# A convolution's tiles moved from GpSimd to VectorE in a two-layer hybrid network on one core

## The chip, the cores and the metric

The kernel runs on one core of one Trainium2 chip, as one launch. The metric is the device time of that launch in microseconds (us), shown as the median of several runs. A profile comes from one execution of its own; its span runs from the first to the last instruction.

## The reference, cut to what matters

The network has two layers over 256 tokens of width 2048, all in float32. The first mixes retention and a sparse attention; the second mixes a depthwise convolution of 31 taps over 1024 channels and an attention over three dilation patterns. The change touches three pieces: the input norm, the convolution and the norm of each head of 128 (`dilated_attention` norms dq and dk so):

```python
def rms_norm(x, gain):
    y = xf * lax.rsqrt(jnp.mean(xf * xf, axis=-1, keepdims=True) + NORM_EPS)
    return y * gain

def conformer_conv(u, g, dw_w, dw_b, ln_g, ln_b):
    a = u * jax.nn.sigmoid(g)
    a = lax.conv_general_dilated(a, dw_w[:, None, :], (1,), [(CONV_K - 1, 0)],
            dimension_numbers=('NWC', 'WIO', 'NWC'), feature_group_count=C) + dw_b
...
def odd_layer(x, norm_g, w_in, ...):
    h = rms_norm(x, norm_g) @ w_in
    cu, cg, cz, dq, dk, dv, dz = split_cols(h, ODD_SPLITS)
    c_out = conformer_conv(cu, cg, ...) * silu(cz)
    d_out = dilated_attention(dq, dk, dv, dil_qn, dil_kn) * silu(dz)
    return x + jnp.concatenate([c_out, d_out], axis=-1) @ w_out
```

## The kernel before, in words

Nearly all of the work is projections: `project` multiplies the normed input, 2048 deep, by 512 columns of weights, in chunks of 512 rows. float32 accuracy is had from three products of two halves: each chunk comes in by one DMA as raw (1 MB), and `prep` (line 92) splits it in two half-chunks of 128x1024, each into an upper part wh, copied by ScalarE (line 104), and a lower part wl, which VectorE subtracts (line 105). TensorE then does wh by xh, wl by xh and wh by xl. Each of raw, wh and wl has three buffers. A half-chunk feeds 24 matmuls of 256 columns (the transposed form, `flip=True`, lines 134 to 136) or 12 of 512 columns (lines 140 to 142). A project of the second layer has four chunks, so eight wh and eight wl.

The input is kept transposed as xT (channels by tokens). `norm_block` (lines 178 to 189) makes its two halves xh and xl, ScalarE and VectorE one instruction for each 256 columns. The root of each token's mean square is not put into them, but into the projections' results: for the first layer `token_rstd` gives rstd1, which `evac_to` (line 266) applies when ScalarE copies a result out of PSUM. Its sums of squares come from `input_squares` (lines 208 to 218), which loads the input a second time, laid out by token (xtok, four DMAs of 512 KB), and lets ScalarE square and sum it. For the second layer they come from `square_block` (lines 191 to 197): a square of four rows of xT on ScalarE and a reduction on VectorE over every 256th element (line 197); `token_squares` adds the four blocks and sums over the channels by two matmuls of one column.

The second layer runs in this order: two projects for the gate and the input of the first four channel tiles of the convolution (cg, cu), two for the second four, six for the queries and keys of the dilated attention (here d projects: d00, d10, d01, d11, d02, d12), three for its values (dv), then three gates and the output. In line 779 GpSimd multiplies input and gate into apad, with 30 zeros ahead, and from then on the first half's convolution can run, beside the projects that follow; the second half's after the fourth project.

`conv` (lines 731 to 754) takes a channel tile and a stretch of taps. Of every four tiles (ct % 4) the first two go to VectorE: one `scalar_tensor_tensor` a tap (line 744) that adds a weighted, shifted apad to a sum in PSUM (cps), each tile in a bank of its own, copied out by ScalarE at the end (line 746). For the other two ScalarE makes the weighted copy (tap, three buffers, line 753) and GpSimd adds it to acc in SBUF (line 754). Tap 0 is written straight into the sum (lines 742, 750). `conv_pieces` cuts a half into 16 pieces of four taps each, of one VectorE tile and one ScalarE/GpSimd tile:

```python
        def piece(i, k):
            def f():
                for ct in (4 * hf + i, 4 * hf + i + 2):
                    conv(ct, k, min(k + CONV_STEP, CONV_K))
            return f
        return [piece(i, k) for i in range(2) for k in range(0, CONV_K, CONV_STEP)]
```

The pieces stand in a list, and `take(range(3))` gives a project one piece after each of its first three chunks. What is left when the last value project has been issued is issued then.

After each d project `head_norm` (lines 269 to 284) squares it on ScalarE, sums each head on VectorE (line 275), has GpSimd make the roots (`rsqrt`, lines 166 to 171) and scales: by VectorE in one multiplication, or, with `act=True`, as for the six d projects, by ScalarE in eight copies of 128 columns (line 281). Then TensorE transposes it (line 293) in two groups of four.

Each engine works its queue in order. The order within it is set by a scheduler that places instructions by its own estimate of times; the weights' loads, splits and evacuations have high priority (`tc.high_priority`), so that the taps fill in between.

Of the kernel before, what the change touches and what calls it, by code (L numbers as in the profile page):

```python
# [33 lines left out]
DILS = (1, 4, 16)  # L34
MMB = 3
WARM = 36
CONV_STEP = 4
HPO = 2000


# [20 lines left out]
def hybrid_kernel(ctx: ExitStack, tc: tile.TileContext, a: dict, out: bass.AP):  # L61
# [143 lines left out]
            nc.tensor.matmul(pt[:, t:t + 1], tot[:, t * 128:(t + 1) * 128], ones, start=True, stop=True)  # L205
        return pt[:, :2]

    def input_squares():

        ss = st.tile([128, 16], F32, name="xss", tag="ss")  # L210
        for t in range(2):
            for c in range(2):
                xt = hp.tile([128, 1024], F32, name="xtok", tag="h")
                nc.sync.dma_start(xt, a["xtok"][:, t, 1024 * c:1024 * c + 1024])
                nc.scalar.activation(xt, xt, AF.Square, accum_out=ss[:, 2 * t + c:2 * t + c + 1])
        tot = st.tile([128, 2], F32, name="xtot")
        nc.vector.reduce_sum(tot, ss[:, :4].rearrange("p (t c) -> p t c", t=2), axis=AX.X)
        return tot

    def token_rstd(tot, name):  # L220

        ms = st.tile([128, 16], F32, name=name + "m", tag="ms")
        nc.vector.tensor_scalar(ms[:, :2], tot, 1.0 / D, EPS, op0=ALU.mult, op1=ALU.add)  # L223
        r = const.tile([128, 2], F32, name=name)
        nc.gpsimd.tensor_tensor(r, ms[:, :2], mhalf[:, :2], op=ALU.pow)  # L225
        return r
# [39 lines left out]
            nc.scalar.activation(dst[:, t, off:off + n], p[:, :n], AF.Copy, scale=r[:, t:t + 1])  # L266
        return f

    def head_norm(view, nh, name, act=False):

        sq = sp.tile([128, 1024], F32, name="sq", tag="sq")
        sqv = sq[:, :2 * nh * 128].rearrange("p (t h d) -> p t h d", t=2, h=nh)
        nc.scalar.activation(sqv, view, AF.Square)
        ss = st.tile([128, 16], F32, name=name + "ss", tag="ss")
        nc.vector.reduce_sum(ss[:, :2 * nh], sq[:, :2 * nh * 128].rearrange("p (g d) -> p g d", d=128), axis=AX.X)
        rs = rsqrt(ss[:, :2 * nh], 2 * nh, HD, name + "rs")
        if act:
            for t in range(2):
                for h in range(nh):
                    i = t * nh + h  # L280
                    nc.scalar.activation(view[:, t, h, :], view[:, t, h, :], AF.Copy, scale=rs[:, i:i + 1])
            return
        rb = rs.rearrange("p (t h) -> p t h", t=2).unsqueeze(3).to_broadcast([128, 2, nh, 128])
        nc.vector.tensor_mul(view, view, rb)

# [19 lines left out]
    def first_block(c):  # L305
        load_block(c)
        if c == 3:
            rstd.append(token_rstd(input_squares(), "rstd1"))

    project(ew[0], 512, lhs, evac_to(hkv), lazy=first_block, cut=load_rest)  # L310
    load_pack("pa")
# [419 lines left out]
    def conv(ct, k0, k1):  # L731


        src, dst = apad[ct // 4][:, ct % 4, :], acc[ct // 4][:, ct % 4, :]
        w, b = dww[:, ct, :], dwb[:, ct:ct + 1]
        if ct % 4 < 2:
            if ct % 4 == 0 and k0 == 0:
                cps[0] = ps.tile([128, 1024], F32, name="cps", tag="sc")
            p = cps[0][:, 512 * (ct % 4):512 * (ct % 4) + S]
            for k in range(k0, k1):  # L740
                if k == 0:
                    nc.vector.tensor_scalar(p, src[:, 0:S], w[:, 0:1], b, op0=ALU.mult, op1=ALU.add)
                else:
                    nc.vector.scalar_tensor_tensor(p, src[:, k:k + S], w[:, k:k + 1], p, op0=ALU.mult, op1=ALU.add)  # L744
            if k1 == CONV_K:
                nc.scalar.copy(dst, p)
            return
        for k in range(k0, k1):
            if k == 0:
                nc.scalar.activation(dst, src[:, 0:S], AF.Identity, scale=w[:, 0:1], bias=b)  # L750
                continue
            tap = sp.tile([128, S], F32, name="tap", tag="tap", bufs=3)
            nc.scalar.activation(tap, src[:, k:k + S], AF.Copy, scale=w[:, k:k + 1])  # L753
            nc.gpsimd.tensor_add(dst, dst, tap)  # L754

    def conv_pieces(hf):
        def piece(i, k):
            def f():
                for ct in (4 * hf + i, 4 * hf + i + 2):
                    conv(ct, k, min(k + CONV_STEP, CONV_K))  # L760
            return f
        return [piece(i, k) for i in range(2) for k in range(0, CONV_K, CONV_STEP)]

    apad, acc = [], []
    for hf in range(2):
# [60 lines left out]
    for p_ in range(3):  # L826
        for i in range(2):
            h = htile(f"d{i}{p_}")
            project(ow[4 + 2 * p_ + i], 512, lhs, evac_to(h, rs=rstd2), extra=take(range(3)))
            head_norm(h.rearrange("p t (h d) -> p t h d", d=128), 4, f"dn{i}{p_}", act=True)  # L830
            T = hp.tile([128, 4, S], F32, name=f"dT{i}{p_}", tag="h")
            dT[i][p_] = T
            for j in range(2):
                pt = transpose4([h[:, t, (2 * j + k) * 128:(2 * j + k + 1) * 128] for k in range(2) for t in range(2)])
                nc.scalar.activation(T[:, 2 * j:2 * j + 2, :].rearrange("p a b -> p (a b)"), pt, AF.Copy,
                                     scale=(dqg, dkg)[i])
# [156 lines left out]
```

## Time and profile before

| | |
|---|---|
| runs shown | 978.9, 979.17 and 979.28 us, median 979.17 |
| profiled execution | 979.7 us |
| its span | 977.9 us |
| TensorE (PE) busy | 953.4 us |
| VectorE (DVE) busy | 607.9 us |
| ScalarE (ACT) busy | 560.8 us |
| GpSimd (POOL) busy | 202.8 us |
| PEld, weight loads beside the matmuls | 870.7 us |

Times are us from the span's start. L104 is line 104 of the kernel. In a row "out<-in" are the names of the tiles, and "128x1024" partitions by elements. A timeline gives start and duration; an "xN" behind a row takes N instructions in a row together. Square brackets give how long the engine stood idle before it and what ended that. A row of a stretch gives its length and then, for PE, PEld, DVE, ACT and POOL in this order, the busy us and the number of instructions; PEclk is the clock granted to TensorE, as a share of the upper of its two levels; behind it stand the share in which the DMA engines were busy and what they moved. Matmul durations overlap, so the distance from one start to the next is what one costs.

### The profile page before, as it was taken

The numbers are of one execution on the slowest core, as the hardware profiler recorded it, in microseconds if no ns is written. First come the engines' busy times: TensorE is split into PE (matmuls) and PEld (weight loads), VectorE is DVE, ScalarE is ACT, GpSimd is POOL, SyncE is SP. The second block draws the span as 40 slices with busy tenths as digits, with TensorE's granted clock in tenths as the row PEclk, the third lists the DMA queues.
The fourth block names the chain that finished last, engine by engine and source line by source line (L and its number), as shares of the span: only waits on it lengthen the run. The fifth ranks groups of instructions, "written<-read, shape, count | busy, mean of one in ns | idle before, by whom it ended". The sixth has DMA issues, their size and how long they took to land.

```text
span 977.9 us, 15775 instructions
## 1 busy us (share of the span) xinstructions
PE 953.4 (97%) x6397; PEld 870.7 (89%) x6397; DVE 607.9 (62%) x837; ACT 560.8 (57%) x839; POOL 202.8 (21%) x194
## 2 busy tenths in 40 slices
PE   9899999999999999999999998999989999999998
PEld 7688989889998998899999986788867789999998
DVE  5666557865744665655684777895855546545643
ACT  6666646655544444543454576666878746765532
POOL 0111100220220010000000599411898302000000
PEclk9999999999999999999999999999999999999999
DMA  8765744345445455545555434554443454443561
GB/s 303 299 241 172 243 172 168 111 150 175 145 149 204 169 173 184 193 167 189 178 186 187 170 144 135 191 192 176 169 172 140 165 212 172 150 148 134 194 210 71
DMA packets 32521, 173.64 MB, mean 178 GB/s; under 512 B 3392, under 2 KB 9664, under 8 KB 13376
## 3 DMA queue, kind: packets, MB, share of 16 engines
q1 hardware_dynamic: 32448, 172.63, 50.2%
q8 instruction: 50, 0.82, 0.3%
q14 instruction: 23, 0.19, 0.1%
HBM read 170.52 MB, written 2.10 MB: 177 GB/s over the span
## 4 chain that ended last, share of the span: by engine, by line
PE 77%; POOL 8%; issue 5%; ACT 3%; DVE 3%; DMA 3%; SPq 0%; POOLq 0%; ACTq 0%
PE mm L134 14%; PE mm L135 14%; PE mm L136 14%; PE mm L141 10%; PE mm L142 10%; PE mm L140 10%; POOL acc L754 7%; DMA raw<-in_ew 1%; DMA xtok<-in_xtok 1%; DVE wl L105 1%; PE tr L293 1%; ACT wh L104 1%; PE dpo L873 1%; PE cmph L357 1%; PE dsc L853 1%
## 5 line engine op out<-in xcount | busy, mean ns | idle before, releaser
L105 DVE TENSOR_TENSOR wl<-raw,wh 128x1024 fp32r<-128x1024 f32 (+2 forms) x326 | 393.6, 1211 | 295.2 <-ACT wh L104 293.1
L104 ACT CAST wh<-raw 128x1024 fp32r<-128x1024 f32 (+2 forms) x326 | 328.0, 1010 | 283.6 <-PE mm L136 169.3
L135 PE MATMUL mm<-xh,wl 128*128 128x256 f32 x1280 | 362.8, 285 | 1.9 <-DVE wl L105 1.9
L134 PE MATMUL mm<-xh,wh 128*128 128x256 f32 x1280 | 360.0, 285 | 1.7 <-ACT wh L104 1.5
L136 PE MATMUL mm<-xl,wh 128*128 128x256 f32 x1280 | 360.5, 284 | 0.0
L135 PEld LDWEIGHTS mm<-xh,wl 128*128 128x128 f32 x1280 | 245.3, 192 | 3.3 <-DVE wl L105 3.1
L134 PEld LDWEIGHTS mm<-xh,wh 128*128 128x128 f32 x1280 | 243.3, 192 | 2.6 <-ACT wh L104 1.9
L136 PEld LDWEIGHTS mm<-xl,wh 128*128 128x128 f32 x1280 | 244.7, 192 | 0.1
L141 PE MATMUL mm<-wl,xh 128*128 128x512 f32 (+1 forms) x608 | 235.0, 388 | 7.3 <-DVE wl L105 7.1
L142 PE MATMUL mm<-wh,xl 128*128 128x512 f32 (+1 forms) x608 | 230.6, 381 | 0.0
L140 PE MATMUL mm<-wh,xh 128*128 128x512 f32 (+1 forms) x608 | 214.0, 385 | 3.0 <-ACT wh L104 2.0
L141 PEld LDWEIGHTS mm<-wl,xh 128*128 128x128 f32 x608 | 114.9, 189 | 35.1 <-DVE wl L105 14.5
L140 PEld LDWEIGHTS mm<-wh,xh 128*128 128x128 f32 x608 | 113.2, 189 | 26.0 <-ACT wh L104 4.0
L142 PEld LDWEIGHTS mm<-wh,xl 128*128 128x128 f32 x608 | 114.8, 189 | 20.2
L754 POOL TENSOR_TENSOR acc<-acc,tap 128x256 f32<-128x256 f32 x120 | 119.1, 993 | 20.7 <-ACT acc L750 6.8
L753 ACT ACTIVATE tap<-apad,pb 128x256 f32<-128x256 f32 x120 | 56.8, 504 | 28.0 <-POOL acc L754 27.5
L744 DVE SCALAR_TENSOR_TENSOR cps<-apad,pb,cps 128x256 f32<-128x256 f32 x120 | 58.4, 486 | 2.5
L225 POOL TENSOR_TENSOR rstd<-rstd2m,mhalf 128x2 f32<-128x2 f32 x1 | 0.7, 697 | 162.3 <-DVE rstd2m L223 162.3
L610 POOL TENSOR_TENSOR rot<-rot,pb 128x512 f32<-128x512 f32 x8 | 11.1, 1404 | 79.7 <-ACT rot L608 79.6
L534 ACT ACTIVATE p<-p,nm 128x128 f32<-128x128 f32 (+1 forms) x32 | 14.2, 445 | 10.7 <-DVE nm L530 10.6
L779 POOL TENSOR_TENSOR apad<-au,sg 128x512 f32<-128x512 f32 x4 | 7.1, 1790 | 35.1 <-DVE au L686 35.1
L703 DVE TENSOR_TENSOR xT<-mm,xT 128x512 f32<-128x512 f32 (+1 forms) x18 | 11.1, 630 | 5.1 <-PE mm L136 5.1
(275 smaller groups left out, 664.0 us busy)
## 6 DMA issues: line engine op xcount, KB each, us to landing
raw<-in_ow SPq DMA_DIRECT2D x64, 1024.0 KB, 4.9
raw<-in_ew SPq DMA_DIRECT2D x53, 1024.0 KB, 4.9
raw<-in_ewo SPq DMA_DIRECT2D x16, 1024.0 KB, 4.9
raw<-in_owo SPq DMA_DIRECT2D x12, 1024.0 KB, 4.9
raw<-in_ewn SPq DMA_DIRECT2D x8, 536.0 KB, 4.1
raw<-in_ew SPq DMA_DIRECT2D x12, 256.0 KB, 4.7
xtok<-in_xtok SPq DMA_DIRECT2D x4, 512.0 KB, 11.7
raw<-in_w1k SPq DMA_DIRECT2D x2, 1024.0 KB, 4.9
```

Of the source, the lines that this page charges most:

```text
L104: nc.scalar.copy(wh[:, k, :n], r)
L105: nc.vector.tensor_sub(wl[:, k, :n], r, wh[:, k, :n].bitcast(F32))
L134: nc.tensor.matmul(o, wh[:, k, cs], xh[:, kk, :], start=first and j == 0, stop=False, **kw)
L135: nc.tensor.matmul(o, wl[:, k, cs], xh[:, kk, :], start=False, stop=False, **kw)
L136: nc.tensor.matmul(o, wh[:, k, cs], xl[:, kk, :], start=False, stop=last, **kw)
L140: nc.tensor.matmul(o, xh[:, kk, ts], wh[:, k, :n], start=first, stop=False)
L141: nc.tensor.matmul(o, xh[:, kk, ts], wl[:, k, :n], start=False, stop=False)
L142: nc.tensor.matmul(o, xl[:, kk, ts], wh[:, k, :n], start=False, stop=last)
L534: nc.scalar.activation(cut(p, b)[t], cut(p, b)[t], AF.Exp, bias=nm[:, i:i + 1], scale=SCALE, accum_out=sm[:, i:i + 1])
L744: nc.vector.scalar_tensor_tensor(p, src[:, k:k + S], w[:, k:k + 1], p, op0=ALU.mult, op1=ALU.add)
L753: nc.scalar.activation(tap, src[:, k:k + S], AF.Copy, scale=w[:, k:k + 1])
L754: nc.gpsimd.tensor_add(dst, dst, tap)
```

## The change

Three things change.

1. *The convolution.* Three of four channel tiles go to VectorE, with their sums side by side at 256 columns in the two banks of one PSUM tile; one goes to ScalarE and GpSimd, with four tap buffers in place of three. The pieces, still 16 a half, carry the VectorE tiles one after the other in steps of five or six taps, and two taps of the GpSimd tile each.
2. *The head norms.* The ScalarE branch of `head_norm` goes: VectorE scales the six d projects too, with one `tensor_mul` of 128x1024 each, both inputs in SBUF, the roots repeated over each head.
3. *The input's squares.* `input_squares` and xtok go; `square_block` and `token_squares` make the sums from xT.

```diff
-    def input_squares():
-        ss = st.tile([128, 16], F32, name="xss", tag="ss")
-        for t in range(2):
-            for c in range(2):
-                xt = hp.tile([128, 1024], F32, name="xtok", tag="h")
-                nc.sync.dma_start(xt, a["xtok"][:, t, 1024 * c:1024 * c + 1024])
-                nc.scalar.activation(xt, xt, AF.Square, accum_out=ss[:, 2 * t + c:2 * t + c + 1])
-        tot = st.tile([128, 2], F32, name="xtot")
-        nc.vector.reduce_sum(tot, ss[:, :4].rearrange("p (t c) -> p t c", t=2), axis=AX.X)
-        return tot
...
-    def head_norm(view, nh, name, act=False):
+    def head_norm(view, nh, name):
...
-        if act:
-            for t in range(2):
-                for h in range(nh):
-                    i = t * nh + h
-                    nc.scalar.activation(view[:, t, h, :], view[:, t, h, :], AF.Copy, scale=rs[:, i:i + 1])
-            return
         rb = rs.rearrange("p (t h) -> p t h", t=2).unsqueeze(3).to_broadcast([128, 2, nh, 128])
         nc.vector.tensor_mul(view, view, rb)
...
         if c == 3:
-            rstd.append(token_rstd(input_squares(), "rstd1"))
+            for b in range(4):
+                square_block(b)
+            rstd.append(token_rstd(token_squares(sqs[0]), "rstd1"))
...
-        if ct % 4 < 2:
+        if ct % 4 < 3:
             if ct % 4 == 0 and k0 == 0:
                 cps[0] = ps.tile([128, 1024], F32, name="cps", tag="sc")
-            p = cps[0][:, 512 * (ct % 4):512 * (ct % 4) + S]
+            p = cps[0][:, S * (ct % 4):S * (ct % 4) + S]
...
-            tap = sp.tile([128, S], F32, name="tap", tag="tap", bufs=3)
+            tap = sp.tile([128, S], F32, name="tap", tag="tap", bufs=4)
...
     def conv_pieces(hf):
-        def piece(i, k):
+        steps = []
+        for i in range(3):
+            e = [round(CONV_K * j / 16 * 3) for j in range(6)]
+            e = sorted(set(min(x, CONV_K) for x in e) | {CONV_K})
+            steps += [(4 * hf + i, x, y) for x, y in zip(e, e[1:])]
+
+        def piece(i):
             def f():
-                for ct in (4 * hf + i, 4 * hf + i + 2):
-                    conv(ct, k, min(k + CONV_STEP, CONV_K))
+                for s_ in steps[i * len(steps) // 16:(i + 1) * len(steps) // 16]:
+                    conv(*s_)
+                conv(4 * hf + 3, 2 * i, min(2 * i + 2, CONV_K))
             return f
-        return [piece(i, k) for i in range(2) for k in range(0, CONV_K, CONV_STEP)]
+        return [piece(i) for i in range(16)]
```

How the engines' queues change shows at three places. The line numbers of the changed kernel are some lower, since lines went; a number behind a tile's name only tells tiles apart.

ScalarE, at the start of the first half's convolution, before (apad is the convolution's input, acc its sum, tap the weighted copy that GpSimd adds):

```order
L104 CAST wh<-raw 128x1024 x8
L750 ACTIVATE acc_5588<-apad_5110,pb 128x256
L753 ACTIVATE tap<-apad_5110,pb 128x256 x3
L750 ACTIVATE acc_5588<-apad_5110,pb 128x256
L104 CAST wh<-raw 128x1024
L753 ACTIVATE tap<-apad_5110,pb 128x256
L104 CAST wh<-raw 128x1024
L753 ACTIVATE tap<-apad_5110,pb 128x256 x3
L104 CAST wh<-raw 128x1024
L753 ACTIVATE tap<-apad_5110,pb 128x256 x3
L104 CAST wh<-raw 128x1024
```

The same place in the change:

```order
L103 CAST wh<-raw 128x1024 x8
L733 ACTIVATE acc_5591<-apad_5113,pb 128x256
L736 ACTIVATE tap<-apad_5113,pb 128x256 x4
L103 CAST wh<-raw 128x1024
L736 ACTIVATE tap<-apad_5113,pb 128x256
L103 CAST wh<-raw 128x1024
L736 ACTIVATE tap<-apad_5113,pb 128x256 x3
L103 CAST wh<-raw 128x1024
L736 ACTIVATE tap<-apad_5113,pb 128x256 x4
L103 CAST wh<-raw 128x1024
L736 ACTIVATE tap<-apad_5113,pb 128x256 x3
```

Tap 0 of a second tile is gone, and the taps between one wh and the next number 4, 1, 3, 4 and on where they numbered 3, 1, 3 and 3.

VectorE in the start, around the reduction for the first layer's root, before (hkv's transposes arrive as tr, blk and bhl are made from them):

```order
L105 TENSOR_TENSOR wl<-raw,wh 128x512
L187 SCALAR_TENSOR_TENSOR xl<-xT,evn,xh 128x256 x4
L105 TENSOR_TENSOR wl<-raw,wh 128x1024 x4
L217 TENSOR_REDUCE xtot<-xss 128x2
L223 TENSOR_SCALAR rstd1m<-xtot 128x2
L105 TENSOR_TENSOR wl<-raw,wh 128x1024
L321 COPY tT<-tr 128x512
L105 TENSOR_TENSOR wl<-raw,wh 128x1024
L321 COPY tT<-tr 128x512
L330 TENSOR_TENSOR blk_383<-tT,pa 128x32x15 x2
L330 TENSOR_TENSOR blk_394<-tT,pa 128x32x15 x2
```

And in the change, where the first three of four reductions over xT's squares (line 196) stand further ahead, among the blocks' xl:

```order
L186 SCALAR_TENSOR_TENSOR xl<-xT,evn,xh 128x256 x4
L196 TENSOR_REDUCE sqs<-sqb 128x256
L104 TENSOR_TENSOR wl<-raw,wh 128x1024 x2
L201 TENSOR_REDUCE sq<-sqs 128x256
L104 TENSOR_TENSOR wl<-raw,wh 128x1024 x2
L210 TENSOR_SCALAR rstd1m<-tr 128x2
L104 TENSOR_TENSOR wl<-raw,wh 128x1024 x2
L304 COPY tT<-tr 128x512 x2
L104 TENSOR_TENSOR wl<-raw,wh 128x1024
L313 TENSOR_TENSOR blk_386<-tT,pa 128x32x15 x2
L313 TENSOR_TENSOR blk_397<-tT,pa 128x32x15 x2
L104 TENSOR_TENSOR wl<-raw,wh 128x1024
```

Three reductions stand in front of the fourth block's xl, and all four in front of the first wl of 128x1024; behind the two copies of tT there is now one wl ahead of blk and one behind.

VectorE in the project after d00, before:

```order
L105 TENSOR_TENSOR wl<-raw,wh 128x1024
L742 TENSOR_SCALAR cps<-apad_5591,pb 128x256
L275 TENSOR_REDUCE dn00ss<-sq 128x8
L744 SCALAR_TENSOR_TENSOR cps<-apad_5591,pb,cps 128x256
L105 TENSOR_TENSOR wl<-raw,wh 128x1024
L744 SCALAR_TENSOR_TENSOR cps<-apad_5591,pb,cps 128x256
L105 TENSOR_TENSOR wl<-raw,wh 128x1024
L744 SCALAR_TENSOR_TENSOR cps<-apad_5591,pb,cps 128x256 x5
```

And in the change (L265 is the scaling of d00):

```order
L104 TENSOR_TENSOR wl<-raw,wh 128x1024
L725 TENSOR_SCALAR cps<-apad_5113,pb 128x256
L262 TENSOR_REDUCE dn00ss<-sq 128x8
L727 SCALAR_TENSOR_TENSOR cps<-apad_5113,pb,cps 128x256
L104 TENSOR_TENSOR wl<-raw,wh 128x1024
L727 SCALAR_TENSOR_TENSOR cps<-apad_5113,pb,cps 128x256
L104 TENSOR_TENSOR wl<-raw,wh 128x1024
L727 SCALAR_TENSOR_TENSOR cps<-apad_5113,pb,cps 128x256
L265 TENSOR_TENSOR d_6140<-d_6140,dn00rs 128x1024
L727 SCALAR_TENSOR_TENSOR cps<-apad_5113,pb,cps 128x256
L104 TENSOR_TENSOR wl<-raw,wh 128x1024
L727 SCALAR_TENSOR_TENSOR cps<-apad_5113,pb,cps 128x256 x2
```

The scaling of d00 stands behind its reduction with two wl and three additions in between, and two wl stand behind it here; the additions go on beside it as before.

## Rows read from the trace of the kernel before

**Rows 1.** Page, part 1: busy us, share of the span and instructions by engine.

```profile
PE 953.4 (97%) x6397; PEld 870.7 (89%) x6397; DVE 607.9 (62%) x837; ACT 560.8 (57%) x839; POOL 202.8 (21%) x194
```

**Rows 2.** Stretch 600 to 620: length, busy by engine, PEclk, DMA share, GB/s.

```profile
600.00:620.00 20.00, 17.35 (x70) 12.75 (x71) 15.12 (x23) 12.10 (x22) 18.98 (x18) 1.00 0.44 158
```

**Rows 3.** Stretch 629.9 to 652; below, VectorE's line L744 alone in it.

```profile
629.90:652.00 22.10, 22.10 (x103) 18.26 (x103) 20.68 (x33) 14.64 (x22) 2.86 (x2) 1.00 0.61 216
...
629.90:652.00 22.10, 11.09 (x23) 1.00 0.61 216
```

**Rows 4.** Waits, 540 to 800 us: total us, times, longest.

```profile
ACT tap L753 <- POOL acc L754: 27.5, 34, 2.3
```

**Rows 5.** Timeline of ScalarE: start, us, what, idle before and releaser.

```profile
577.46 1.03 ACT L104 CAST wh<-raw 128x1024 fp32r<-128x1024 f32 x1
...
580.78 1.03 ACT L104 CAST wh<-raw 128x1024 fp32r<-128x1024 f32 x1
...
584.93 1.03 ACT L104 CAST wh<-raw 128x1024 fp32r<-128x1024 f32 x1
```

**Rows 6.** Timeline of ScalarE, 546 to 553 us.

```profile
546.48 1.05 ACT L104 CAST wh<-raw 128x1024 fp32r<-128x1024 f32 x1 [1.83 <-PE mm L136]
550.22 0.60 ACT L750 ACTIVATE acc<-apad,pb 128x256 f32<-128x256 f32 x1 [2.69 <-POOL apad L779]
...
552.42 1.03 ACT L104 CAST wh<-raw 128x1024 fp32r<-128x1024 f32 x1
```

**Rows 7.** Page, part 5 (busy, mean ns); then line L754 (min/median/max ns).

```profile
L105 DVE TENSOR_TENSOR wl<-raw,wh 128x1024 fp32r<-128x1024 f32 (+2 forms) x326 | 393.6, 1211 | 295.2 <-ACT wh L104 293.1
...
L754 POOL TENSOR_TENSOR acc<-acc,tap 128x256 f32<-128x256 f32 x120 | 119.1, 993 | 20.7 <-ACT acc L750 6.8
...
L754 POOL TENSOR_TENSOR acc<-acc,tap x120: 722/740/1817, 551.3 to 759.2; 128x256 f32<-128x256 f32 x120
```

**Rows 8.** Timeline of VectorE at 545.8 us.

```profile
545.83 1.35 DVE L686 TENSOR_TENSOR au<-mm,rrow 128x512 f32<-128x512 f32 x2
```

**Rows 9.** Timeline of ScalarE: evacuations of d projects one to three, and of dv0.

```profile
624.38 0.69 ACT L266 ACTIVATE d<-mm,rstd 128x512 f32<-128x512 f32 x1 [0.88 <-PE mm L142]
...
647.20 0.69 ACT L266 ACTIVATE d<-mm,rstd 128x512 f32<-128x512 f32 x1 [0.53 <-PE mm L142]
...
669.91 0.69 ACT L266 ACTIVATE d<-mm,rstd 128x512 f32<-128x512 f32 x1 [0.53 <-PE mm L142]
...
771.20 0.69 ACT L266 ACTIVATE dv<-mm,rstd 128x512 f32<-128x512 f32 x1 [0.78 <-PE mm L142]
```

**Rows 10.** Chain of waits, 124 to 130 us: start, us, what.

```profile
126.84 0.87 PE tr L293 x8
```

**Rows 11.** Timeline of TensorE at the seventh wh of the first half.

```profile
571.87 0.50 PE L134 MATMUL mm<-xh,wh 128*128 128x256 f32 x2 [0.95 <-ACT wh L104]
```

**Rows 12.** Timeline of GpSimd: the root of the first d project.

```profile
631.49 2.66 POOL L170 TENSOR_TENSOR dn00rs<-dn00rsm,mhalf 128x8 f32<-128x8 f32 x1
```

**Rows 13.** Timeline of TensorE in the start: three of its stops.

```profile
25.96 0.50 PE L141 MATMUL mm<-wl,xh 128*128 128x512 f32 x1 [0.52 <-DVE wl L105]
...
35.47 0.44 PE L293 MATMUL tr<-pa,hkv 128*128 128x128 f32 x2 [1.54 <-ACT hkv L266]
...
46.33 0.50 PE L141 MATMUL mm<-wl,xh 128*128 128x512 f32 x1 [1.05 <-DVE wl L105]
```

**Rows 14.** Line L197: min/median/max ns, first and last start.

```profile
L197 DVE TENSOR_REDUCE sqs<-sqb x4: 1995/2000/2016, 432.6 to 503.4; 128x256 f32<-128x1024 f32 x4
```

**Rows 15.** Timeline of VectorE in the start.

```profile
9.49 0.48 DVE L187 SCALAR_TENSOR_TENSOR xl<-xT,evn,xh 128x256 fp32r<-128x256 f32 x1
...
10.53 0.48 DVE L187 SCALAR_TENSOR_TENSOR xl<-xT,evn,xh 128x256 fp32r<-128x256 f32 x1
...
24.68 2.36 DVE L105 TENSOR_TENSOR wl<-raw,wh 128x1024 fp32r<-128x1024 f32 x2 [1.45 <-ACT wh L104]
```

**Rows 16.** Timeline of VectorE: a reduction over adjacent elements.

```profile
629.91 1.21 DVE L275 TENSOR_REDUCE dn00ss<-sq 128x8 f32<-128x1024 f32 x1
```

More of the change, by code (lines that the diff above doesn't have):

```diff
@@ L36 @@
 WARM = 36
-CONV_STEP = 4
 HPO = 2000
@@ L829, in hybrid_kernel @@
             project(ow[4 + 2 * p_ + i], 512, lhs, evac_to(h, rs=rstd2), extra=take(range(3)))
-            head_norm(h.rearrange("p t (h d) -> p t h d", d=128), 4, f"dn{i}{p_}", act=True)
+            head_norm(h.rearrange("p t (h d) -> p t h d", d=128), 4, f"dn{i}{p_}")
             T = hp.tile([128, 4, S], F32, name=f"dT{i}{p_}", tag="h")
@@ L951 @@
     arr["xT"] = A(x.T.reshape(KT, 128, S).transpose(1, 0, 2))
-    arr["xtok"] = A(x.reshape(2, 128, D).transpose(1, 0, 2))
     arr["ev_norm"] = A(i["ev_norm"][0].reshape(KT, 128).T)
```

## The prediction

> **What bounds the kernel now.** I read the page's totals first, then the busy time by stretch, then the waits, then the stretches line by line. TensorE is busy 97% of the span [rows 1], and the granted clock is 1.00, the upper level, in every stretch read: the matmuls leave nothing to win, and but for two products of one column the change leaves them alone. Only stretches in which TensorE waits count. From 600 to 620 us it is busy for only 17.35 [rows 2], from 630 to 652 for the whole 22.10 [rows 3]: the loss sits where ScalarE and GpSimd work on the convolution's taps. The waits say why: 34 times, 27.5 us in all, a tap on ScalarE stood still until an addition on GpSimd freed its buffer [rows 4].
>
> The reader should follow one turn of that ring. ScalarE works its queue in order, and the wh copies that TensorE needs stand behind the taps. Behind three taps a wh comes 3.32 us after the last one, behind four 4.15 [rows 5]. TensorE uses one up in 2.88 us in the transposed projects: 1.05 of a copy and 1.83 of waiting for TensorE, just before the convolution [rows 6]. The ring's pace is GpSimd's. An addition takes 740 ns at the median and 993 in the mean [rows 7]: of three in a row one is stretched by some 0.85 us, the one that meets VectorE's wl.
>
> **What that costs now.** From the first au of the first half to the first evacuation of the first d project 78.55 us pass [rows 8, 9]. Two projects of eight wh at 2.88 and one of 21.8 (a d project's 22.71 [rows 9] less its eight transposes, 0.87 in a group like them [rows 10], which come later) make 67.9: 10.6 lost in the first half. From the third d project's evacuation to the first dv's 101.29 us pass, where four projects at 22.71 make 90.8: 10.4 lost in the second half [rows 9]. Nearly all that can be won is in these 21 us.
>
> **The change part by part.** My sum goes against the profiled execution's own 979.7 us (span 977.9), 0.5 above the median of the three runs.
>
> *First half of the convolution.* GpSimd keeps one tile of four, so of the 120 taps 60 go, and 30 stay in each half. In the new order the first ten wh stand behind 4, 1, 3, 4, 3, 3, 4, 3, 3 and 2 taps; after them come runs of wh with none. The stretch begins as it did: ScalarE stands 2.69 us for apad, and the next wh comes 5.94 us after the last, 3.06 late [rows 6], which TensorE does not feel, since copies run ahead of it by about that much. The seventh wh then stands behind 22 taps where it stood behind 20; with four tap buffers it waits for the 18th addition and not the 17th, comes 0.8 later than now, and TensorE, which waits 0.95 us there [rows 11], waits 1.8. The next two intervals of 3.33 add 0.45 each, the tenth nothing: 2.7. Bounds: 0, if the lead is larger than it looks, and 5, half of today's loss.
>
> *Second half.* Four taps go ahead early, and 26 stand between nine wh. Up to the ninth GpSimd does 25 additions, at 3.33 us for three 27.8 us, and one root, 2.66 [rows 12]: 30.5. TensorE wants these eight wh in one project's time, 22.7. Of the 7.8 left over the lead hides some 3; the new scaling, of wl's shape, can stretch one addition more, 0.9. I take 5.5 lost. Bounds: 2 and 8. The halves together give back 10.6 - 2.7 + 10.4 - 5.5 = 12.8 us.
>
> *The early taps of the second half* wait for its apad as the first ones did, in front of seven wh: 3.06 late again, with the lead only partly regained. Between nothing and 3.1 I take 1.0, because VectorE's load by wh there (one wl, two or three additions) is below 2.88 us and regains some.
>
> *VectorE takes over.* It gets 62 additions more at 482 ns (11.09 us for 23 [rows 3]), 30 us, and six scalings. A d project then holds eight wl, some 21 additions, the reduction and the scaling. The trace has no scaling of d on VectorE; nearest is wl, the same shape with both inputs in SBUF: 1.21 [rows 7]. Between the first two reductions of now lie eight wl, 23 additions and one reduction: VectorE is busy for 20.68 of 22.10 us and TensorE for all of them [rows 3]. Two additions less and a scaling more are 0.25 more: 20.9 in a project of 22.7. It costs nothing while nothing in the queue waits; what covers it is the lead of wl before its matmuls. The scaling stands three additions and two wl behind its reduction, some 3.7 us, and the root needs 2.66 [rows 12] and the ways. Where GpSimd still has taps, VectorE waits with wl behind. The second half's sums also need the first's bank copied out, by a ScalarE that may stand at a transpose. Bounds 0 and 3; I take 1.0. ScalarE's 48 scalings by head and its 60 taps give nothing on their own: where they stood it had idle time, or waited in the ring.
>
> [...]
>
> *The input's squares.* Four loads of 512 KB, four squares and a small reduction go, and with them the stop of 1.54 us before the first transposes [rows 13], whose input is scaled by the root that waited for them. Four squares of xT on ScalarE, four reductions and one of the totals on VectorE and two small products come. The reduction has L197's shape and stride: 2.00 us [rows 14]. VectorE's chain now decides. From the third chunk's xl, over at 9.97 [rows 15], with the square done by some 10.3, come four reductions (7.8, each starting a little before the last has ended), eight pairs of wl and xl at 1.04 from xl to xl [rows 15] (8.3), a wl of 0.6 and four xl (1.6): the fourth block's first wl starts near 28.6 instead of 24.68 [rows 15]. TensorE, which waited for it until 25.96 [rows 13], loses 3.9. It wins back the 1.54; the two products and a matmul more ahead of the transposes cost 0.5; and the stop of 1.05 before 46.33 [rows 13] goes, as the new order puts one wl ahead of the blk and another between them and the bhl. Net 3.9 + 0.5 - 1.5 - 1.1 = 1.8 slower. Bounds: -2 (the squares hidden in full) and 3.3 (the longer stop stays). The loads' absence wins nothing else: the fourth block's weights stand ahead of them in SP's queue.
>
> [...]
>
> Sum: 979.7 - 12.8 + 1.0 + 1.0 + 1.8 = 970.7; on the scale of the median **970.2 us**.
>
> **The rivals.**
> *VectorE becomes the bound: slower.* Its queue is in order and now carries the weights' lower halves, three conv tiles and the scalings. If each scaling waits for a root that stands behind taps, and wl are stretched, a d project grows from 22.7. It decides from about 25.6 a project: six times 2.9 is the 9.0 forecast and the 8.2 of ring stalls that it would hide. At 26.5 the time is 970.2 + 6 x 3.8 - 8.2 = 985. For it: VectorE goes to some 95% of six projects in a row. Against: the 22.10 us at 20.68 busy that stalled nobody [rows 3]. Chance 0.10.
> *The ring stays.* The groups of 3 and 4 taps are as dense as before where they stand. If the lead is not regained, the halves lose 5 and 8, and the early taps 3: 970.2 + 2.3 + 2.5 + 2 = 977, at the middle of these 975. For it: each group costs the same 3.3 to 4.2. Chance 0.19.
> *The lead hides it all.* The halves lose 0 and 2, the start and the early taps nothing: 970.2 - 2.7 - 3.5 - 1.8 - 1 = 961. For it: runs of seven wh without a tap in between. Chance 0.13.
> [...] L197's row is against it: 0.03.
> *The change does not do what it says.* Half of the taps go, but ScalarE's queue is held as long by other waits (apad, the copies out of PSUM), and the start eats the rest: 979. Chance 0.06.
>
> **How the numbers follow.** My forecast, 970.2, has 0.49: own range 966 to 974. About 0.2% (2 us) is what a measurement of this kernel can tell from no change. Faster by more, below 977.2: 0.49 + 0.19 + 0.13 + 0.03, less 0.02 for a ring at its end: 0.82. Within: 0.06 and those 0.02: 0.08. Slower: 0.10. The range of 8 in 10 reaches from 961.5 to 977.0: it takes in the ring and nearly all of the hidden lead.
>
> **What would show it.** Right: the taps' wait for additions falls from 27.5 us to under 12; the first au to first d evacuation take about 71 us, the four projects behind the third d evacuation about 96; the fourth block's first wl starts near 28.6, and the first transposes come near 38. Wrong: VectorE without idle time from 630 to 760 us with TensorE waiting on wl (first rival); reductions L196 below 1.5 us; or a scaling L265 that waits several us for its root.

## The result, and the profile after

The changed kernel takes 967.86 us in the median (966.9 to 968.18, 4 runs), the kernel before 979.22 (978.9 to 980.06, 4 runs): a ratio of 0.9881, interval 0.9864 to 0.9898. The forecast was 970.2, with 961.5 to 977.0 as its range.

The starts and evacuations that the prediction spoke of are, in the changed kernel, these rows of the timelines of VectorE (the first, against [rows 8]) and ScalarE (the others, against [rows 9]):

```profile
548.07 0.68 DVE L669 TENSOR_TENSOR au<-mm,rrow 128x512 f32<-128x512 f32 x1
```

```profile
618.31 0.69 ACT L253 ACTIVATE d<-mm,rstd 128x512 f32<-128x512 f32 x1 [0.53 <-PE mm L141]
...
663.63 0.69 ACT L253 ACTIVATE d<-mm,rstd 128x512 f32<-128x512 f32 x1 [0.48 <-PE mm L141]
...
758.88 0.69 ACT L253 ACTIVATE dv<-mm,rstd 128x512 f32<-128x512 f32 x1 [0.53 <-PE mm L141]
```

They cut the execution in five stretches. This table gives them for both kernels and for all of the experiments, from the same rows of each trace; the next section says what the kernels are.

| kernel | to the first au | first half: to d00 | d00 to d01 | second half: to dv0 | to the end | median, us |
|---|---|---|---|---|---|---|
| before | 545.83 | 78.55 | 45.53 | 101.29 | 206.72 | 979.22 |
| the change | 548.07 | 70.24 | 45.32 | 95.25 | 207.32 | 967.86 |
| conv_only | 547.24 | 70.28 | 45.43 | 95.47 | 207.50 | 966.09 |
| old_squares | 547.45 | 70.27 | 45.32 | 95.24 | 207.59 | 966.83 |
| act_scaling | 549.47 | 70.28 | 45.43 | 95.46 | 207.22 | 969.46 |
| square_by_token | 547.55 | 70.23 | 45.33 | 95.26 | 207.32 | 966.70 |
| no_taps | 548.45 | 67.39 | 45.32 | 90.62 | 207.22 | 960.78 (one run) |
| before_four_buffers | 545.93 | 80.23 | 43.88 | 100.62 | 206.73 | 979.16 (one run) |
| taps_on_gpsimd | 547.70 | 67.39 | 50.06 | 96.11 | 207.23 | 970.70 |
| four_tiles_vector | 547.42 | 67.45 | 45.26 | 98.63 | 217.55 | 978.21 |
| paced_taps | 548.24 | 67.39 | 45.32 | 90.93 | 207.14 | 960.79 |
| paced_taps_gpsimd_squares | 546.44 | 67.39 | 45.32 | 90.93 | 207.13 | 959.48 |
| paced_late_sums | 546.09 | 67.39 | 45.32 | 90.97 | 207.14 | 958.47 |
| paced_old_squares | 546.21 | 67.39 | 45.32 | 90.93 | 207.41 | 959.00 |

Where nothing in them is changed, the three stretches in the middle repeat within 0.1 us from kernel to kernel and the last within 0.5; the first varies by more than a microsecond, and the last section says with what. So the halves are read from the traces, and the start with care. The medians come from sets of runs taken apart from each other, and in these sets the kernel before took between 979.22 and 981.25 us; each ratio below is against the kernel before in the same set.

The change won 8.3 us in the first half and 6.0 in the second, 0.2 between them, and lost 2.2 in the start and 0.6 at the end; why the end is longer was not looked into. In the busy time by stretch, the project behind d00 runs without a stop as the stretch of [rows 3] did, though VectorE has the scaling too; what the second half still loses stands in one project, the 27.14 us before d02's evacuation, with GpSimd busy for 25.41:

```profile
618.31:640.98 22.67, 22.67 (x105) 18.85 (x104) 19.83 (x29) 12.10 (x15) 2.86 (x2) 1.00 0.55 186
...
686.71:713.85 27.14, 25.00 (x108) 19.03 (x107) 20.31 (x26) 19.99 (x36) 25.41 (x25) 1.00 0.42 148
```

In the first half TensorE's stops of more than 0.2 us are two. The first is the seventh wh's, 1.31 us where [rows 11] have 0.95; behind the second, at 580.32, no other follows before d00's evacuation:

```profile
574.92 0.51 PE L133 MATMUL mm<-xh,wh 128*128 128x256 f32 x2 [1.31 <-ACT wh L103]
...
580.32 0.39 PE L134 MATMUL mm<-xh,wl 128*128 128x256 f32 x1 [0.58 <-DVE wl L104]
```

The waits from 540 to 800 us have the ring of [rows 4] with half its cost (the prediction asked for under 12), and the page's part 5 has an addition at 1001 ns in the mean, near the 993 of [rows 7]:

```profile
ACT tap L736 <- POOL acc L737: 14.0, 18, 1.8
```

```profile
L737 POOL TENSOR_TENSOR acc<-acc,tap 128x256 f32<-128x256 f32 x60 | 60.1, 1001 | 14.0 <-ACT acc L733 8.4
```

In the start, VectorE's timeline has the reductions at the predicted price and the fourth block's first wl at 27.95 where 28.6 was forecast; on TensorE one stop of 2.86 us (its row is in the last section) takes the place of the three in [rows 13]. The first transposes come at 39.42, where the prediction looked for 38:

```profile
10.18 2.03 DVE L196 TENSOR_REDUCE sqs<-sqb 128x256 f32<-128x1024 f32 x1 [0.28 <-ACT sqb L195]
...
26.16 1.90 DVE L196 TENSOR_REDUCE sqs<-sqb 128x256 f32<-128x1024 f32 x1
27.95 2.37 DVE L104 TENSOR_TENSOR wl<-raw,wh 128x1024 fp32r<-128x1024 f32 x2
```

### The profile page after: what moved, and what is told of

The parts are those of the page before. It is cut to its first block, busy times and chain, and to the rows that moved or that the text cites. A ratio compares the mean times of both kernels' runs of the same rounds, so it can differ in the third digit from the quotient of the medians.

```text
span 966.2 us, 15609 instructions
## 1 busy us (share of the span) xinstructions
PE 950.3 (98%) x6401; PEld 873.3 (90%) x6401; DVE 649.0 (67%) x909; ACT 521.1 (54%) x727; POOL 146.1 (15%) x134
## 4 chain that ended last, share of the span: by engine, by line
PE 88%; POOL 4%; ACT 3%; DVE 3%; issue 1%; DMA 0%; SPq 0%; POOLq 0%; ACTq 0%
PE mm L134 14%; PE mm L133 14%; PE mm L135 14%; PE mm L140 12%; PE mm L141 12%; PE mm L139 12%; POOL acc L737 3%; ACT wh L103 1%; PE tr L274 1%; DVE wl L104 1%; PE dpo L864 1%; PE dsc L844 1%; PE cmph L340 1%; DMA raw<-in_ew 0%; PE tr L529 0%
## 5 line engine op out<-in xcount | busy, mean ns | idle before, releaser
L140 PEld LDWEIGHTS mm<-wl,xh 128*128 128x128 f32 x608 | 115.2, 190 | 31.5 <-DVE wl L104 10.6
L727 DVE SCALAR_TENSOR_TENSOR cps<-apad,pb,cps 128x256 f32<-128x256 f32 x180 | 87.5, 486 | 3.5
L737 POOL TENSOR_TENSOR acc<-acc,tap 128x256 f32<-128x256 f32 x60 | 60.1, 1001 | 14.0 <-ACT acc L733 8.4
L736 ACT ACTIVATE tap<-apad,pb 128x256 f32<-128x256 f32 x60 | 28.4, 503 | 16.9 <-POOL acc L737 14.0
L517 ACT ACTIVATE p<-p,nm 128x128 f32<-128x128 f32 (+1 forms) x32 | 14.2, 446 | 10.7 <-DVE nm L513 10.6
L196 DVE TENSOR_REDUCE sqs<-sqb 128x256 f32<-128x1024 f32 x8 | 16.0, 2004 | 0.3 <-ACT sqb L195 0.3
```

What stands on the lines that cost most here:

```text
L140: nc.tensor.matmul(o, xh[:, kk, ts], wl[:, k, :n], start=False, stop=False)
L196: nc.vector.reduce_sum(sqs[0][:, b, :], sq.rearrange("p k s -> p s k"), axis=AX.X)
```

## The experiments

**Which part of the change does what.** Four kernels undo or do one part. conv_only has the convolution alone. Against the changed kernel two calls differ, and what they call comes back (shown in part):

```diff
+            rstd.append(token_rstd(input_squares(), "rstd1"))
...
+            head_norm(h.rearrange("p t (h d) -> p t h d", d=128), 4, f"dn{i}{p_}", act=True)
```

> The convolution's part of the change alone (three tiles of four on VectorE, one on GpSimd, four tap buffers); the input's squares and the d projects' scaling as in the kernel before. Theory: the gain is the shorter ring of taps. The first half gives back 8.3 us and the second about 6, and the start costs nothing: 979.2 - 14.3 = 965 us, the first hkv evacuation near 34.7 as before. Rival (the scaling on VectorE is what freed ScalarE): without it the halves give back less than 10 us, so 969 or more.

It took 966.09 us, ratio 0.9864 (0.9849 to 0.9879). Its halves are those of the change within 0.3 us: all that was won is the convolution's. Its start is that of the kernel before, yet the first au came at 547.24 and not 545.83: a start varies by that much with nothing in it changed.

old_squares puts back `input_squares` alone.

> The changed kernel with the input's squares as before (xtok loaded and squared on ScalarE); all else changed. Theory: the reductions on VectorE cost the 2.2 us by which the first au came later (548.07 against 545.83), so 967.9 - 2.2 = 965.7, with the first transposes waiting again for the root. Rival (the four loads less pay elsewhere, or the start's delay is hidden later): 967.9 or above.

It took 966.83 (ratio 0.9868, 0.9850 to 0.9886), 1 us from the change and with overlapping intervals. The first au came at 547.45, 0.6 earlier than in the change and not 2.2: between the theory and the rival, and the difference lies inside what the start varies by.

act_scaling puts back the eight copies on ScalarE alone.

> The changed kernel with the six d projects scaled by ScalarE as before, in eight copies each. Theory: the scaling is worth nothing by itself in either place, but for one addition of GpSimd that it no longer stretches (0.9 us at most): 967 to 968.5. Rival one (VectorE at its bound is relieved): 965 or less. Rival two (ScalarE's copies stand before wh copies, and the change gained by taking them away): 970 or more.

The time, 969.46 (ratio 0.9890, 0.9874 to 0.9905), is near the second rival's, but the trace says otherwise: from the first au to the end it needs 418.4 us, the change 418.1. The rest is its start, where TensorE's granted clock was low for twice as long (last section). The scaling is worth 0.2 to 0.3 us, on VectorE's side. That GpSimd's additions would be freed of a stretch did not show: the second half is 95.46 with the scaling on ScalarE and 95.25 with it on VectorE (a few taps stand differently).

square_by_token lets ScalarE write the squares so that VectorE reads adjacent elements:

```diff
-        sq = hp.tile([128, 4, S], F32, name="sqb", tag="h")
-        nc.scalar.activation(sq, xT[:, 4 * b:4 * b + 4, :], AF.Square)
-        nc.vector.reduce_sum(sqs[0][:, b, :], sq.rearrange("p k s -> p s k"), axis=AX.X)
+        sq = hp.tile([128, S, 4], F32, name="sqb", tag="h")
+        nc.scalar.activation(sq.rearrange("p s k -> p k s"), xT[:, 4 * b:4 * b + 4, :], AF.Square)
+        nc.vector.reduce_sum(sqs[0][:, b, :], sq, axis=AX.X)
```

> The changed kernel, but ScalarE writes the squares with the four channels of a token side by side, so that the reductions read adjacent elements; the order on every engine stays. Theory: the reduction costs 1.2 us in place of 2.0 because of its stride, four of them give 3.2 us back to VectorE's chain, and the stop of 3.03 us before the fourth block's second product nearly goes: 967.9 - 2.8 = 965. Rival one: ScalarE's strided write takes twice as long (2 us instead of 1), delays the xh behind it, and the start is no faster: 967 to 969. Rival two: the reduction takes 2.0 us whatever the stride: 967.9.

966.70 us (ratio 0.9865, 0.9847 to 0.9883), the first au at 547.55. Both halves of the question have a clear answer, in the rows of the two lines (min/median/max ns):

```profile
L196 DVE TENSOR_REDUCE sqs<-sqb x8: 1219/1220/1220, 11.4 to 506.0; 128x256 f32<-128x1024 f32 x8
...
L195 ACT ACTIVATE sqb<-xT x8: 2005/2075/2119, 9.3 to 503.8; 128x1024 f32<-128x1024 f32 x8
```

The reduction's 2.0 us is its stride, as [rows 14, 16] had it (2.00 and 1.21). But the stride went to ScalarE, whose square took 1.05 us in the change and takes 2.08 now. The first rival's mechanism holds: the wl of the fourth block comes at 27.58, 0.4 earlier.

**Is it the ring, and what of it is left?** no_taps leaves out the copies and additions of taps 1 to 30 of the fourth tile.

> The changed kernel without taps 1 to 30 of the tile that ScalarE and GpSimd work (neither the weighted copies nor the additions; this part of the convolution is left out). Theory: what TensorE still loses in the two halves is the ring alone. From the first au to the first d evacuation 67.9 us (70.24 in the changed kernel), from the third d evacuation to dv0's 90.7 (95.25), so the span is shorter by about 7. Rival (VectorE's added work costs part of it): the two stretches stay above 69 and 93.

The first half fell to 67.39 and the second to 90.62, the theory's numbers: what the change still loses in the halves, 2.85 and 4.63 us, is the taps' alone, and VectorE's 62 more additions and six scalings, which this kernel keeps, cost the halves nothing.

before_four_buffers tries the tap buffers by themselves, in the kernel before (`bufs=3` to `bufs=4`).

> The kernel before with four tap buffers in place of three, nothing else. Theory: the pace is GpSimd's and a buffer more only lets ScalarE run one tap further ahead: the first half takes 78.55 us give or take 1, the second 101.3 give or take 1.5, the time stays at 979. Rival (the fourth buffer is what the change won by): the halves fall by 4 us or more each.

80.23 and 100.62 us, 979.16 in all; ScalarE's wait for additions was 27.2 us against 27.5 [rows 4]. The first half is 0.7 us outside the theory's bound and the stretch behind it shorter by as much as the half is longer (43.88 against 45.53). From the first au to dv0 it took 224.73 us against 225.37: by itself the fourth buffer won next to nothing. What it is worth beside the change's 30 taps a half was not run.

**Two ways without the ring.** taps_on_gpsimd moves the weighted copy to GpSimd:

```diff
-            nc.scalar.activation(tap, src[:, k:k + S], AF.Copy, scale=w[:, k:k + 1])
+            nc.gpsimd.tensor_scalar(tap, src[:, k:k + S], w[:, k:k + 1], None, op0=ALU.mult)
```

> The changed kernel with the weighted copy of each tap on GpSimd too, so that no wh copy stands behind a tap. Theory: with ScalarE's queue free of the ring the first half takes 67.9 us and the second about 91 as without taps, and the time is 961 to 962. Rival one: GpSimd needs twice the time, the roots of the d projects stand behind taps in its queue, and VectorE waits for them with wl behind: above 968. Rival two: its reads stretch VectorE's wl, and the first half stays at 70.

970.70 us (ratio 0.9900, 0.9884 to 0.9917). The ratio's interval overlaps that of the change; from the first au to the end the trace needs 420.8 us where the change needs 418.1. The first half is at its floor, 67.39, so there the ring is gone and VectorE is not held up; what it costs later is the first rival's mechanism, a wait that takes the place of the ring. On VectorE's timeline d00's sum starts at 619.48, and the scaling waits 7.27 us for the root; on GpSimd's the root's first step stands behind taps until 629.67; TensorE then stops 2.70 us before the transposes, and its granted clock is 0.69 from 632 to 636 us and 0.89 to 640. With both, the stretch from d00 to d01 is 4.7 us longer (50.06 against 45.32), and a like stop of 2.65 us stands at 731.40, in the second half:

```profile
619.48 1.21 DVE L262 TENSOR_REDUCE dn00ss<-sq 128x8 f32<-128x1024 f32 x1
...
631.65 1.23 DVE L265 TENSOR_TENSOR d<-d,dn00rs 128x1024 f32<-128x1024 f32 x1 [7.27 <-POOL dn00rs L169]
```

```profile
627.76 1.83 POOL L736 TENSOR_SCALAR tap<-apad,pb 128x256 f32<-128x256 f32 x2
629.67 0.20 POOL L168 TENSOR_SCALAR dn00rsm<-dn00ss 128x8 f32<-128x8 f32 x1
629.95 1.67 POOL L169 TENSOR_TENSOR dn00rs<-dn00rsm,mhalf 128x8 f32<-128x8 f32 x1
```

```profile
632.93 1.49 PE L274 MATMUL tr<-pa,d 128*128 128x128 f32 x8 [2.70 <-DVE d L265]
```

four_tiles_vector gives VectorE all four tiles (`ct % 4 < 4`, four tiles of 31 taps in the pieces, none for GpSimd).

> The changed kernel with all four tiles on VectorE (31 taps more in each half, 4 x 256 columns of PSUM) and none on ScalarE and GpSimd. Theory: the ring is gone, VectorE has 30 us more to do, and since it was idle for 17 us of 759 to 806 and for 30 of 806 to 870 the work moves there: 961 to 963. Rival (VectorE is at its bound in the d projects, wl come late): a d project takes over 23.5 us where it takes 22.7, and the time is 968 or more.

978.21 us (ratio 0.9975, 0.9966 to 0.9984): the rival's time, but by another way than late wl. Five of the six d projects do not exceed 22.7 us, with VectorE busy for 21.35 of 22.66 in the one shown here; the fifth, up to d02's evacuation, takes 32.05:

```profile
637.47:660.13 22.66, 22.66 (x105) 18.84 (x104) 21.35 (x32) 12.09 (x15) 2.85 (x2) 1.00 0.54 186
```

The loss stands where one PSUM tile changes hands. ScalarE's copy of the first half's last sum waits for VectorE's late additions, and the evacuation of d02 and the wh behind it wait in its queue; TensorE stops for 4.97 us, and from 716 to 720 us its granted clock is 0.50. Behind the second half's sums, which are now over at 808, stands the dilated attention's product dsc in the same PSUM tile. The last stretch is 10 us longer: TensorE waits there at dsc and, the longest, for an evacuation of dv, with a clock of 0.52 from 820 to 824. On ScalarE's and TensorE's timelines:

```profile
714.56 0.37 ACT L729 COPY acc<-cps 128x256 f32<-128x256 f32 x1 [6.94 <-DVE cps L727]
714.83 1.27 ACT L253 ACTIVATE d<-mm,rstd 128x512 f32<-128x512 f32 x2
```

```profile
715.58 0.80 PE L139 MATMUL mm<-wh,xh 128*128 128x512 f32 x1 [4.97 <-ACT d L253]
...
808.68 0.94 PE L843 MATMUL dsc<-dT,dT 128*128 128x128 f32 x6 [1.00 <-ACT acc L729]
...
818.87 0.58 PE L133 MATMUL mm<-xh,wh 128*128 128x256 f32 x1 [4.60 <-ACT dv L253]
```

**The ring's spacing.** paced_taps keeps every instruction, buffer and engine of the change and alters the order alone, by two edits. A tap may not be queued on ScalarE ahead of the wh that it is tied to (whs collects the wh copies as they are made), and the fourth tile's taps go into the first eight pieces of a half, four in each, in place of two in each of 16:

```diff
-            nc.scalar.activation(tap, src[:, k:k + S], AF.Copy, scale=w[:, k:k + 1])
+            with tc.issue_after(whs[-2 + (k - k0) // 2].ins):
+                nc.scalar.activation(tap, src[:, k:k + S], AF.Copy, scale=w[:, k:k + 1])
...
-                conv(4 * hf + 3, 2 * i, min(2 * i + 2, CONV_K))
+                if i < 8:
+                    conv(4 * hf + 3, 4 * i, min(4 * i + 4, CONV_K))
```

> The changed kernel with the order of ScalarE's queue alone made different: no two taps of the GpSimd tile are issued before the wh copy that they are tied to, so that after the first four groups two taps stand behind a wh where three or four stood. The same instructions, buffers and engines. Theory: what the changed kernel still loses in the halves (2.9 and 4.6 us against the run without taps) is taps standing too close in ScalarE's queue; GpSimd's pace of some 1.1 us an addition fits two into 2.7 to 2.9 us. First half 67.4 to 68.5, second 90.7 to 92, the time 961 to 962. Rival (the roots of d11 and d02 behind additions, or wl stretched by them, cost it whatever the spacing): the second half stays above 94 and the time at 965 or more.

960.79 us (ratio 0.9790, 0.9777 to 0.9804), the halves 67.39 and 90.93: all of the ring's 7.5 us but 0.3 is won, with the same 60 taps, and the roots still between GpSimd's additions. Where the change has three or four taps before a wh, the first half's queue here has at most two behind the first four groups. The second half's early taps stand behind d01 in place of ahead of d00, and its taps reach on into the project behind d02. No run separates the two edits, so what won is the looser order that they make together. On ScalarE's timeline the evacuations that bound the stretches are:

```profile
615.63 0.69 ACT L254 ACTIVATE d<-mm,rstd 128x512 f32<-128x512 f32 x1 [0.53 <-PE mm L142]
...
660.95 0.69 ACT L254 ACTIVATE d<-mm,rstd 128x512 f32<-128x512 f32 x1 [0.48 <-PE mm L142]
...
751.88 0.69 ACT L254 ACTIVATE dv<-mm,rstd 128x512 f32<-128x512 f32 x1 [0.53 <-PE mm L142]
```

ScalarE's wait for additions is down to 5.6 us, and now GpSimd waits for taps:

```profile
POOL acc L739 <- ACT tap L738: 15.5, 10, 4.5
...
ACT tap L738 <- POOL acc L739: 5.6, 8, 1.2
```

**The start.** paced_taps_gpsimd_squares adds up the first layer's squares on GpSimd:

```diff
+            eng.tensor_add(sq[:, 0:2, :], sq[:, 0:2, :], sq[:, 2:4, :])
+            eng.tensor_add(sqs[0][:, b, :], sq[:, 0, :], sq[:, 1, :])
```

> The same with the first layer's four reductions over squares replaced by two additions each on GpSimd (128x512 and 128x256), which is idle there. Theory: VectorE's chain to the fourth block's first wl loses its four reductions of 2.0 us, the stop of 2.9 us there and the lower clock behind it go, and the first au comes 2 to 4 us earlier than in the changed kernel (548.07): 958 to 960. Rival (GpSimd's additions and VectorE's wl hold each other up, or the weights of the second project come too late anyway): the first au stays at 547 or later, and the time within 1 of the paced kernel.

959.48 us (ratio 0.9783, 0.9770 to 0.9797); the first au at 546.44, 1.8 earlier than in paced_taps. The stop is 2.23 us and not gone: VectorE's instructions take longer beside GpSimd's additions here. On VectorE's timeline the four xl of the fourth block take 3.19 us beside two additions, and 1.69 in the change, where GpSimd is idle:

```profile
23.23 3.19 DVE L187 SCALAR_TENSOR_TENSOR xl<-xT,evn,xh 128x256 fp32r<-128x256 f32 x4
26.34 2.35 DVE L105 TENSOR_TENSOR wl<-raw,wh 128x1024 fp32r<-128x1024 f32 x2
```

paced_late_sums leaves two blocks to GpSimd and queues the reductions of the other two behind the fourth block's two wl.

> The paced kernel with the first layer's sums of squares placed by hand: two blocks' additions on GpSimd, the other two reductions on VectorE, each behind one of the two wl of the fourth block instead of in front of them. Theory: the stop of 2.2 to 2.9 us before the fourth block's second product came from reductions (or additions that stretch VectorE) ahead of its wl; behind them they stand in VectorE's slack, no stop there is over 1 us, the granted clock stays at 1.00, and the first au comes at 544 to 545.5: 956.5 to 958.5. Rival (the reductions only move the stop to the wl behind them): the first au at 546 or later, 959 or more.

958.47 us (ratio 0.9774, 0.9759 to 0.9790), the lowest median of all, though its interval overlaps those of the other paced kernels, and inside the theory's range; no stop from 8 to 50 us is over 0.6 us and the granted clock stays at 1.00. But the first au comes at 546.09, not before 545.5: five stops of a quarter to half a microsecond take the place of one, so the rival has a part of it.

paced_old_squares has the old start beside the paced taps.

> The paced kernel with the first layer's squares as in the kernel before (xtok loaded again). Theory: the old start costs a stop before the transposes and one before blk, together 2 to 2.6 us, the new one a stop of 2.9 and a lower clock: the old is better by 1 to 2 us, 959 to 960. Rival (2 MB of loads less are worth more than the stop): 961 or more.

959.00 us (ratio 0.9783, 0.9767 to 0.9799), as the theory had it, the first au 2 us ahead of paced_taps', though the intervals of the two overlap. The squares where the input lies gain nothing in the form that the change gives them: ahead of the fourth block's wl the reductions cost up to 2 us, and placed behind them they draw level with the second load of the input.

## Why the prediction was right

*The bound and the place.* Right: the ring on ScalarE's queue was the loss, and it was worth 11.2 and 10.7 us (78.55 - 67.39, 101.29 - 90.62) where the working had 10.6 and 10.4.

*First half.* Right: 2.85 us lost where 2.7 was worked out from the 18th addition in place of the 17th. The seventh wh comes 0.8 us later than before, as worked out, counted from the first ScalarE instruction on apad (21.38 us against 20.57); the stop in front of it is 1.31 us and not 1.8, and the rest was lost in smaller pieces.

*Second half.* Right in kind, a little too large: 4.63 for 5.5. The 0.9 for a stretched addition is the part that no run confirms; in act_scaling, without the scaling on VectorE, the second half took 95.46 us where the change takes 95.25. The loss stands where the working put it, in the project with d11's root among the additions.

*Early taps and VectorE's load.* The two terms of 1.0 each were not there. The early taps stand in the project before d00's evacuation, where a wh comes at 603.07, 5.41 us after the last, and TensorE has no stop of more than 0.2 us from 580.32 to 618: the lead of the copies covers it. For VectorE's load, d00 to d01 takes 45.32 us, and 45.32 without taps too; VectorE, busy for 19.83 of 22.67 us there, holds nobody up, as [rows 3] had shown. With a fourth tile its wl were not late either, but its sums were. The forecast lies 2.3 us above the median for these reasons: the two terms made 2.0 where 0.2 was won, and the halves gave back 1.6 more than the 12.8 worked out; against that stand 0.4 more lost in the start and the 0.6 at the end, for which the sum had no term (2.7 together on the profiled executions).

*The start.* 2.24 us for 1.8, by another sum. The chain of reductions came out (27.95 for 28.6), the two old stops went as forecast, but the new stop brought a lower clock with it, which the working did not have; without it the start would by that have come out some 0.6 slower. That 2.24 lies so near 1.8 is in part luck: one profile of each kernel has the first au at 545.83 to 547.45 in the five with the old start, and at 547.42 to 549.47 in the six with the new one. The 0.03 set against L197's row was for shorter reductions: the change's L196 take 1.90 to 2.07 us, and 1.22 only where square_by_token lets them read adjacent elements.

*The rival that ends on the other side* fell by its own test: no d project but the one with the ring, 27.14 us, exceeds 23.1. What it warned of, a root behind taps, needs a fuller GpSimd queue, and taps_on_gpsimd shows it.

*VectorE beside GpSimd.* In the trace of the kernel before, the 53 of GpSimd's 120 additions that meet no wl take 722 to 748 ns; the 33 that share 0.9 us or more with one, which has two inputs in SBUF, take 1.34 to 1.82 us. In the change five of the six scalings of d, also with two inputs in SBUF, take 1.22 us; d11's, at 700.00 with additions beside it, takes 1.75. The four xl go from 1.69 to 3.19 us beside GpSimd's additions in paced_taps_gpsimd_squares. The convolution's own additions on VectorE, with their sum in PSUM, take 486 ns in the mean in both kernels' pages and never more than 492, with GpSimd adding beside them.

## What to carry to other kernels

Where a copy that the bottleneck waits for shares an in-order queue with filler work, count how many fillers stand between two such copies and compare their partner engine's pace with the bottleneck's. Here a looser order of them won all but 0.3 us of what leaving them out won, with no instruction saved; a buffer more, or a faster place for some of them, won less or nothing. And before an engine is freed of filler work, look at what else stands in the new engine's queue (roots) and in the resource that it then holds longer (a PSUM tile).

## What the runs showed of the hardware

In these traces TensorE's granted clock falls for a few microseconds after some stops: in the change it is 0.50 in place of 1.00 from 29.8 to 33.2 us, behind a stop of 2.86. Most of what the runs of the kernel before and of paced_taps differ by goes with it. In the busy time by stretch (24 to 36 us of the change, PEclk third from last):

```profile
24.00:28.00 4.00, 2.21 (x9) 1.18 (x7) 4.00 (x8) 0.59 (x1) 0.00 (x0) 1.00 1.00 370
28.00:32.00 4.00, 2.76 (x8) 2.21 (x9) 4.00 (x4) 1.05 (x1) 0.00 (x0) 0.72 0.46 127
32.00:36.00 4.00, 4.00 (x18) 3.23 (x16) 2.53 (x3) 1.05 (x1) 0.00 (x0) 0.85 0.57 231
```

and on TensorE's timeline, the matmuls behind the stop:

```profile
29.24 0.50 PE L140 MATMUL mm<-wl,xh 128*128 128x512 f32 x1 [2.86 <-DVE wl L104]
29.57 0.43 PE L141 MATMUL mm<-wh,xl 128*128 128x512 f32 x1
29.81 0.63 PE L139 MATMUL mm<-wh,xh 128*128 128x512 f32 x1
30.23 0.63 PE L140 MATMUL mm<-wl,xh 128*128 128x512 f32 x1
30.66 0.63 PE L141 MATMUL mm<-wh,xl 128*128 128x512 f32 x1
```

From 29.81 on they start 0.43 us apart, at a granted clock of 0.50 (29.81 to 33.2 us), where 0.23 is the distance at 1.00 (20 to 24 us); eight of them cost 1.6 us. In act_scaling's profile, with the same stop of 2.85 us, 28 to 32 and 32 to 36 us were granted 0.58 and 0.57, which is twice the price. The runs' own times go with their mean clock: paced_taps took 958.92 us at a mean granted clock of 1.000 and 960.47 to 960.82 in its four runs at 0.998. The kernel before is not free of it: in the comparison with paced_taps its runs at 0.998 took 980.70 to 981.84 us, and those at 0.999 or 1.000 979.42 to 979.54. Later in the execution it follows the stops of 2.70 us in taps_on_gpsimd and of 4.97 and 4.60 us in four_tiles_vector, so that a part of what these two lose is the clock's. Which stops it follows is not settled here: the profile of conv_only shows the lower clock (0.76 from 24 to 28 us) behind a stop of 1.79 us, that of paced_old_squares keeps 1.00 behind one of 2.17.

The second thing is the price of a stride, in square_by_token's rows and [rows 14, 16]: VectorE's reduction over 1024 elements goes from 1.22 to 2.00 us when it reads every 256th element, ScalarE's square from 1.05 to 2.08 when it writes every fourth. The runs show what these two forms cost, and not why.
